# A hybrid decoder step on one core: grouped table matmuls, a regrouped state-space schedule, and unscaled query norms with fused scores

## The chip, the cores and the metric

The kernel runs on one core of one Trainium2 chip. It is written engine by engine: TensorE (PE in the profile) multiplies, VectorE (DVE), ScalarE (ACT) and GpSimd (POOL) work on tiles, SyncE (SP) issues most DMAs. Every engine works through its own queue in order, and semaphores make an instruction wait for what it reads or overwrites. The metric is the device time of one launch in microseconds.

## What is computed

One inference step of a decoder layer for 256 prompt positions and 8 x 4 sample positions, 288 columns in all, in float32:

```python
x = x + 0.5 * swiglu(rms_norm(x), w_gate, w_up, w_down)  # FFN 1
z = rms_norm(x) @ w_in  # columns: ssm u | q | k | v
# SSM: 64 groups x 16 channels, 64 complex states a group
lam_bar = exp(lam * dt);  B_bar = ((lam_bar - 1) / lam) * B
h[t] = lam_bar * h[t-1] + B_bar u[t];  y = gelu(Re(C h) + D u)
y = y * sigmoid(y @ w_glu)
# attention: 16 query heads, 4 key heads, window 128, one sink a head
q = rms_norm(q); k = rms_norm(k)
logits = where(valid, q k^T / 8 - slope * distance, -inf)
m = max(max(logits), sink)
p = exp(logits - m); o = (p @ v) / (sum(p) + exp(sink - m))
x = x + w_out @ concat(rms_norm(y_ssm), rms_norm(o))
x = x + 0.5 * swiglu(rms_norm(x), ...)  # FFN 2
```

The two norms in front of q can be joined: q's own norm divides by the root mean square of a head, so a common factor of the token (R, the norm of the layer's input) drops out of everything but the epsilon.

## The kernel before

**Bulk work.** All large products go through `mm3` (L290 to L292): the weights are split into a high part `wh` (ACT, L124) and a low part `wl` (DVE, L125), and each k tile takes three matmuls of 288 columns. The weights come as *pieces* in one list; a piece is used in one *slot* (24 matmuls in the projections). While TensorE works on a slot, the next pieces are split two slots ahead and loaded six ahead (`raw`, SP's queue).

**Side work.** Everything else is hung between the pieces. `W.at(slot, f)` runs f in the queue order of that slot; `W.spread(slot, generator)` runs one step of a generator a slot, up to each `yield`. So the engines' queues are written by this list, and an instruction of a later slot never overtakes one of an earlier slot on its engine. Small products use tiles of one PSUM pool, eight tiles named `main`, in rotation with the bulk work.

**Tables.** During FFN 1, `precompute` builds the SSM's matrices for eight j, one tile a turn, with `tile_tables` (L620 to L636): four transposes (L623) into a PSUM tile, a copy, a step; the same again; then one product of 128 rows by 256 columns (L629), of which only four diagonal blocks of 32 rows by 64 columns are used and copied out one by one (L636).

**The mixing stage** begins at slot `base`. Slots base to base+39 hold w_in: key 0, then the eight SSM blocks j (two slots each, from base+2), key 1, the values, and the query blocks i = 0 to 7 (from base+24); w_out follows from base+40.

An SSM block j passes through these steps, each in a slot of its own relation to s = base+2j+5: its input is stored to DRAM (`ud`, from ACT's queue) and loaded back in another layout (`ssm_u_load`, tile `U`, four DMAs of 36 KB, L767); its matrices come by `ssm_load_a` (`ma`, 512 KB, L771), `ssm_load_r` (`rot`, L775) and `ssm_load_b` (`mb`, 768 KB, L789), all in SP's queue; `ssm_state` multiplies (L798), rotates with `rot` on DVE (L804 to L807), scans (L814), rotates back (L820 on POOL, L821 on DVE); `ssm_out` multiplies again (L833). Then come the gate (`ssm_glu`, L856) and the split of the result for w_out (`y_split`, L737 to L747).

**Attention.** A query block i (two heads) is scaled by R out of PSUM (`qn`, L1171, DVE), squared (`q_square`, L1007, ACT), and summed by small matmuls (`sums`, L1025). `row_rsqrt` (L970 to L976) takes the reciprocal root on POOL, for two blocks at once. `scores` multiplies with the keys (L1043), scales by that root on ACT (L1049), adds the distance bias on DVE (L1053), takes the maximum (L986, L987), the exponentials on ACT (L994) and the final scale on DVE (L1002). `probs_t` transposes (L1062), `pv` multiplies with the values (L1075) and copies the head out (L1079). `sample` does the same for the 32 sample tokens (L1093 to L1142).

The slots of the attention's steps are written by hand, in relation to S, the slot at which block i's query is there (`probs_t` at S+9, `pv` at S+11).

## Time and profile before

| what | value |
|---|---|
| median of three runs | 1873.59 us (1873.23 to 1874.56) |
| the profiled execution | 1872.55 us |
| its span | 1870.7 us |
| TensorE busy | 1852.7 us (99%) |
| DVE, ACT, POOL busy | 1211.4, 852.0, 249.7 us |

In the trace FFN 1 runs to about 806 us, the mixing stage from there to about 1060, and FFN 2 after it. "Waits" below are idle times of an engine, put down to the instruction that released it. In the chain of work that ended last, a row is the start, the length and the instruction or DMA. In a group of instructions the columns are line, engine, operation, output and inputs, shapes and count, then the busy time and the mean of one in ns, then the idle time before it. A float32 matmul other than a transpose shows as two records.

### The profile page before, as it was taken

Reading aid. Unit: us, or ns where it says so; the run is one execution under the profiler, and the core shown is the slowest. Engines: PE = TensorE matmul, PEld = TensorE weight load, DVE = VectorE, ACT = ScalarE, POOL = GpSimd, SP = SyncE. Lnnn points to the kernel's source line nnn. Section 1 sums busy time; section 2 is a strip of 40 time slices with the busy share of each in tenths; the row PEclk is TensorE's granted clock in tenths of the full one; section 3 lists DMA queues with packets and bytes.
Section 4 is the critical chain, followed back from the end, with each engine's and each line's share of the span. In section 5 each row is a group of like instructions: output and inputs, shape, how many; then the busy total and the mean of one; then the engine's idle time right before and its main releaser. Section 6 shows DMA issues by size and latency. Waiting matters only on the chain.

```text
span 1870.7 us, 38190 instructions
## 1 busy us (share of the span) xinstructions
PE 1852.7 (99%) x15620; PEld 1836.0 (98%) x15620; DVE 1211.4 (65%) x1893; ACT 852.0 (46%) x1347; POOL 249.7 (13%) x324
## 2 busy tenths in 40 slices
PE   9999999999999999999989999999999999999999
PEld 9999999999999999998989999999999999999999
DVE  6677667666667755688888885555555555555555
ACT  6444444444444444643576554443444334434433
POOL 3201011000100100211214740000000000000000
PEclk9999999999999999999999999999999999999999
DMA  7555656557655764788734455556555565556555
GB/s 278 199 181 163 219 181 212 193 164 234 207 197 154 235 214 148 234 296 293 237 123 140 157 181 183 179 159 189 191 179 168 171 197 180 162 169 208 180 161 161
DMA packets 122624, 359.08 MB, mean 192 GB/s; under 512 B 22064, under 2 KB 30256, under 8 KB 121264
## 3 DMA queue, kind: packets, MB, share of 16 engines
q1 hardware_dynamic: 114496, 340.48, 56.7%
q10 hardware_dynamic: 7952, 16.16, 2.5%
q8 instruction: 122, 2.00, 0.4%
q14 instruction: 54, 0.44, 0.1%
HBM read 338.40 MB, written 20.22 MB: 192 GB/s over the span
## 4 chain that ended last, share of the span: by engine, by line
PE 92%; DVE 3%; DMA 2%; issue 1%; ACT 1%; POOL 1%; SPq 0%; DVEq 0%; ACTq 0%; POOLq 0%
PE main L290 30%; PE main L292 30%; PE main L291 30%; DVE wl L125 1%; DMA U<-ud 1%; DMA ud<-t 0%; DMA raw<-in_w_in 0%; DMA yd<-yg 0%; PE main L623 0%; PE main L629 0%; ACT wh L124 0%; PE main L833 0%; PE main L1062 0%; DVE sm_m L986 0%; POOL x L1178 0%
## 5 line engine op out<-in xcount | busy, mean ns | idle before, releaser
L125 DVE TENSOR_TENSOR wl<-raw,wh 128x1024 fp32r<-128x1024 f32 (+2 forms) x677 | 753.5, 1113 | 442.9 <-ACT wh L124 441.2
L290 PE MATMUL main<-xh,wh 128*128 128x288 f32 x3136 | 903.5, 288 | 0.4 <-ACT xh L216 0.3
L292 PE MATMUL main<-xh,wl 128*128 128x288 f32 x3136 | 898.6, 287 | 0.7 <-DVE wl L125 0.6
L291 PE MATMUL main<-xl,wh 128*128 128x288 f32 x3136 | 898.1, 286 | 0.9 <-DVE xl L217 0.9
L124 ACT CAST wh<-raw 128x1024 fp32r<-128x1024 f32 (+2 forms) x677 | 637.2, 943 | 493.3 <-PE main L291 332.7
L290 PEld LDWEIGHTS main<-xh,wh 128*128 128x128 f32 x3136 | 593.4, 189 | 3.6 <-ACT xh L216 0.8
L291 PEld LDWEIGHTS main<-xl,wh 128*128 128x128 f32 x3136 | 593.4, 189 | 1.9 <-DVE xl L217 1.5
L292 PEld LDWEIGHTS main<-xh,wl 128*128 128x128 f32 x3136 | 593.4, 189 | 1.7 <-DVE wl L125 0.8
L290 PE MATMUL main<-hh,wh 128*128 128x288 f32 x1664 | 477.8, 287 | 0.0
L291 PE MATMUL main<-hl,wh 128*128 128x288 f32 x1664 | 476.0, 286 | 0.6 <-DVE hl L743 0.6
L292 PE MATMUL main<-hh,wl 128*128 128x288 f32 x1664 | 476.0, 286 | 0.0
L291 PEld LDWEIGHTS main<-hl,wh 128*128 128x128 f32 x1664 | 314.5, 189 | 1.0 <-DVE hl L743 0.8
L290 PEld LDWEIGHTS main<-hh,wh 128*128 128x128 f32 x1664 | 314.5, 189 | 0.3
L292 PEld LDWEIGHTS main<-hh,wl 128*128 128x128 f32 x1664 | 314.5, 189 | 0.2 <-DVE wl L125 0.2
L364 POOL TENSOR_TENSOR s<-s,R 128x288 f32<-128x288 f32 x88 | 70.5, 801 | 1139.7 <-ACT s L363 1139.7
L373 ACT CAST hh<-h 128x288 fp32r<-128x288 f32 x88 | 38.0, 432 | 222.3 <-DVE h L372 222.3
L363 ACT ACTIVATE s<-t 128x288 f32<-128x288 f32 x88 | 39.0, 443 | 219.5 <-DVE t L362 219.5
L394 DVE SCALAR_TENSOR_TENSOR x<-main,x 128x288 f32<-128x288 f32 x128 | 58.4, 456 | 39.8 <-PE main L292 39.4
L372 DVE TENSOR_TENSOR h<-main,s 128x288 f32<-128x288 f32 x88 | 40.1, 456 | 55.2 <-PE main L292 54.9
L362 DVE TENSOR_TENSOR t<-main,R 128x288 f32<-128x288 f32 x88 | 40.1, 456 | 44.9 <-PE main L292 44.6
L374 DVE TENSOR_TENSOR hl<-h,hh 128x288 fp32r<-128x288 f32 x88 | 40.4, 459 | 43.8 <-ACT hh L373 43.8
L1178 POOL TENSOR_TENSOR x<-x,t 128x288 f32<-128x288 f32 x32 | 47.8, 1499 | 52.0 <-DVE t L1177 51.2
(262 smaller groups left out, 818.1 us busy)
## 6 DMA issues: line engine op xcount, KB each, us to landing
raw<-in_w_gu SPq DMA_DIRECT2D x349, 512.0 KB, 4.1
raw<-in_w_dn SPq DMA_DIRECT2D x128, 384.0 KB, 3.1
raw<-in_w_dn SPq DMA_DIRECT2D x128, 320.0 KB, 3.2
raw<-in_w_in SPq DMA_DIRECT2D x40, 512.0 KB, 4.7
raw<-in_w_out SPq DMA_DIRECT2D x32, 512.0 KB, 3.5
...
ma<-mats SPq DMA_DIRECT2D x8, 512.0 KB, 5.7
```

The costliest lines, as they stand in the source:

```text
L124: self.nc.scalar.copy(wh[:, :n], t[:, :n])
L125: self.nc.vector.tensor_tensor(wl[:, :n], t[:, :n], wh[:, :n].bitcast(F32), op=ALU.subtract)
L290: pe.matmul(ps, wh[:, s], woven(rh[k]), start=first and a == 0, stop=False)
L291: pe.matmul(ps, wh[:, s], woven(rl[k]), start=False, stop=False)
L292: pe.matmul(ps, wl[:, s], woven(rh[k]), start=False, stop=last and a == n - 1)
L362: dve.tensor_tensor(t1, pg[:, :N], R, op=ALU.mult)
L363: act.activation(s1, t1, AF.Silu)
L364: pool_e.tensor_tensor(s2, s1, R, op=ALU.mult)
L372: dve.tensor_tensor(halved(h), evens(pu[:, :N]), evens(s2), op=ALU.mult)
L374: dve.tensor_tensor(hl, h, hh.bitcast(F32), op=ALU.subtract)
L394: dve.scalar_tensor_tensor(x[d], ps[:, :N], 0.5, x[d], op0=ALU.mult, op1=ALU.add)
L1178: eng.tensor_tensor(x[d], x[d], t, op=ALU.add)
```

## The change

**Tables.** One group a tile: eight transposes into two PSUM tiles, then the product as eight matmuls of 32 output rows and 64 columns, each onto its own column tile (its 32 PSUM partitions), so that only the diagonal blocks are computed. One copy takes all four blocks. A tile takes two steps fewer.

**SSM.** State j is one piece later and stands between the same two pieces as out j-2, ahead of it. `ma` and `rot` of j > 1 are loaded one slot later than before, and U ahead of them. DVE's four products of 256 columns become two of 512; POOL's product (L820) goes to DVE; the subtraction and addition follow in the same step. Two gate blocks run in the same slots. The SSM's norm starts in the same slot, with one step a slot where it had two.

**Attention.** q is no longer scaled by R: DVE copies it out of PSUM, and ACT squares it from PSUM. The epsilon then has to carry the token's sum of squares, which `eps_rows` puts in place (three matmuls of two columns, some small copies). `bias` writes distance times slope, divided by the root, on ACT, in four copies a head block, from SBUF. `scores` comes two slots later (i even) or three (i odd); one fused DVE operation a part adds that bias to the PSUM scores, multiplies by the root, and takes the maximum with the sink. Four of them, each with a read of its maximum, replace ACT's four scaling copies and DVE's two additions, two reductions and one maximum.

```diff
@@ -617,23 +617,21 @@
+            pss = [pa.tile([P, 512], F32, name="main") for _ in range(3)]
             for i in range(2):
-                ps = pa.tile([P, 512], F32, name="main")
                 for q_ in range(4):
-                    pe.transpose(ps[:, q_ * P:(q_ + 1) * P],
+                    pe.transpose(pss[i][:, q_ * P:(q_ + 1) * P],
                                  bed[i][:, q_].rearrange("p j g c -> p (j g c)"), ident)
-                act.copy(stage[:, i].rearrange("p q m -> p (q m)"), ps)
-                yield
-            ps = pa.tile([P, 512], F32, name="main")
             for i, xx in ((0, xr), (1, xi)):
-                pe.matmul(ps[:, :256], rep[i].rearrange("p q g c -> p (q g c)"), xx[:, :, 1:5, :],
-                          start=i == 0, stop=i == 1)
+                for q_ in range(4):
+                    pe.matmul(pss[2][32 * q_:32 * q_ + 32, :64], rep[i][:, q_].rearrange("p g c -> p (g c)"),
+                              xx[:, q_, 1:5, :], start=i == 0, stop=i == 1)
+            act.copy(stage[:, 0].rearrange("p q m -> p (q m)"), pss[0])
             yield
-            for q_ in range(4):
-                pp = slice(32 * q_, 32 * q_ + 32)
-                act.copy(kk[pp].rearrange("p n d -> p (n d)"), ps[pp, 64 * q_:64 * q_ + 64])
+            act.copy(kk.rearrange("p n d -> p (n d)"), pss[2][:, :64])
...
+    def eps_rows():
+
+        a = acc.rearrange("p (j t) -> p j t", j=T)
+        pool_e.tensor_copy(vT[:, 0, :SEQ].rearrange("p (b j k) -> p j b k", b=2, j=T),
+                           a[:, :, NB:].rearrange("p j (b k) -> p j b k", b=2))
+        r = vT[:, 1, :P].rearrange("p (b g j) -> p j g b", b=NB, g=4)
+        for j in range(T):
+            pool_e.tensor_copy(r[:, j], a[:, j, None, :NB].to_broadcast([P, 4, NB]))
+        yield
+        ps = aux()
+        for b, rows in enumerate((vT[:, 0, :P], vT[:, 0, P:SEQ], vT[:, 1, :P])):
+            pe.matmul(ps[:, 2 * b:2 * b + 2], rows, e["ones"][:, :2], start=True, stop=True)
+        v = mp.tile([P, 6], F32, name="eps_v")
+        ts(v, ps[:, :6], EPS / D, EPS * EPS, op0=ALU.mult, op1=ALU.add)
+        yield
+        pool_e.tensor_copy(eps_q[:, 0:4], v[:, 0:4])
+        pool_e.tensor_copy(eps_q[:, 4:10], v)
...
-        br, bi = b[0][:, :, NB:], b[1][:, :, NB:]
-        co, si = rot[:, :, 0, :], rot[:, :, 1, :]
-        z, w = (sa.tile([P, 2, 4, NCH], F32, name="r" + n, bufs=2) for n in "zw")
+        both = [P, 2, 4, NCH]
+        cosi = rot.rearrange("p q s k -> p s q k")
+        co, si = cosi[:, 0], cosi[:, 1]
+        z, w = (sa.tile(both, F32, name="r" + n, bufs=2) for n in "zw")
         q = slice(4 * j, 4 * j + 4)
-        tt(z[:, 1], br, co, op=ALU.mult)
-        tt(w[:, 1], bi, si, op=ALU.mult)
-        tt(z[:, 0], bi, co, op=ALU.mult)
-        tt(w[:, 0], br, si, op=ALU.mult)
-        yield
+        for r, v in ((z, b[0]), (w, b[1])):
+            tt(r, v[:, None, :, NB:].to_broadcast(both), cosi, op=ALU.mult)
         for i in range(2):
             tt(fin_s[:, i, q, :], b[i][:, :, :NB], fin_s[:, i, q, :], op=ALU.add)
-        tt(z[:, 1], z[:, 1], w[:, 1], op=ALU.add)
-        tt(z[:, 0], z[:, 0], w[:, 0], op=ALU.subtract)
+        yield
+        tt(z[:, 0], z[:, 0], w[:, 1], op=ALU.add)
+        tt(z[:, 1], w[:, 0], z[:, 1], op=ALU.subtract)
         for i in range(2):
             dve.tensor_tensor_scan(flat(w[:, i]), flat(D0[j % 2]), flat(z[:, i]), 0.0, op0=ALU.mult, op1=ALU.add)
         yield
         cs = CS[j % 2]
-        for i in range(2):
-            act.copy(cs[:, i, :, :NB], e["h0"][:, 1 - i, q, :])
-        both = [P, 2, 4, NCH]
-        pool_e.tensor_tensor(z, w, si[:, None].to_broadcast(both), op=ALU.mult)
+        act.copy(cs[:, :, :, :NB], e["h0"][:, :, q, :])
+        tt(z, w, si[:, None].to_broadcast(both), op=ALU.mult)
         tt(cs[:, :, :, NB + 1:], w, co[:, None].to_broadcast(both), op=ALU.mult)
-        yield
-        tt(cs[:, 1, :, NB + 1:], cs[:, 1, :, NB + 1:], z[:, 0], op=ALU.subtract)
-        tt(cs[:, 0, :, NB + 1:], cs[:, 0, :, NB + 1:], z[:, 1], op=ALU.add)
+        tt(cs[:, 0, :, NB + 1:], cs[:, 0, :, NB + 1:], z[:, 1], op=ALU.subtract)
+        tt(cs[:, 1, :, NB + 1:], cs[:, 1, :, NB + 1:], z[:, 0], op=ALU.add)
+        yield
         act.copy(fin[:, :, q], cs[:, :, :, W1])

...
+    W.spread(base + 4, eps_rows())
...
-        W.at(s + 1 if j > 1 else base + 1 + j, ssm_load_a, j)
-        W.at(s + 1 if j > 1 else base + 2 + j, ssm_load_r, j)
         W.at(s + 2, ssm_u_load, j)
-        W.at(s + 2, ssm_decay, j)
-        W.spread(s + 4, ssm_state(j), True)
+        W.at(s + 2 if j > 1 else base + 1 + j, ssm_load_a, j)
+        W.at(s + 2 if j > 1 else base + 2 + j, ssm_load_r, j)
+        W.at(s + 3, ssm_decay, j)
         W.at(s + 6, ssm_load_b, j)
-        W.at(s + 9, ssm_out, j)
-        if j % 2:
-            W.at(s + 10, ssm_y_store, j // 2)
-            W.at(s + 11, ssm_y_load, j // 2)
-            W.spread(s + 13, ssm_glu(j - 1))
-            W.spread(s + 14, ssm_glu(j))
-    W.at(s + 8, state_done)
-    W.at(s + 17, ssm_done)
-
...
+    for j in range(10):
+        s = base + 2 * j + 10
+        if j < 8:
+            W.spread(s, ssm_state(j))
+        if j > 1:
+            W.at(s, ssm_out, j - 2)
+        if j in (3, 5, 7, 9):
+            y = (j - 3) // 2
+            W.at(s + 1, ssm_y_store, y)
+            W.at(s + 2, ssm_y_load, y)
+            s += 6 if y < 3 else 5
+            W.spread(s, ssm_glu(2 * y))
+            W.spread(s, ssm_glu(2 * y + 1))
+    W.at(base + 28, state_done)
+    W.at(base + 36, ssm_done)
+    W.spread(base + 38, e["norm"](e["ones"], acc, R_ssm, 1.0 / 1024, 4 * EPS))
...
-    def q_square(i):
-        qb = QN[i]
-        sq = mp.tile([P, SEQ], F32, name="qsq", bufs=2)
-        act.activation(sq, qb, AF.Square)
-        QN[i] = (qb, sq)
-        p, g = divmod(i, 4)
-        if g == 3:
-            s2 = mp.tile([P, P], F32, name="qssq")
-            qs = QS[p][0].rearrange("p b g j -> p (b g j)")
-            act.activation(s2, qs, AF.Square)
-            act.activation(qs, qs, AF.Copy, scale=qg)
-            QS[p] = (qs, s2)
+    def q_scale(p):
+        qs = QS[p].rearrange("p b g j -> p (b g j)")
+        act.activation(qs, qs, AF.Copy, scale=qg)
...
-        ts(v, ps[:, :cols], 1.0 / 64, EPS, op0=ALU.mult, op1=ALU.add)
-        RQ[m] = row_rsqrt(v, cols)
+        stt(v, ps[:, :cols], 1.0 / 64, eps_q[:, :cols], op0=ALU.mult, op1=ALU.add)
+        vs = mp.tile([P, 8], F32, name="rq_s", bufs=2)
+        tt(vs, v[:, :8], nsl[:, 8 * m:8 * m + 8], op=ALU.mult)
+        o = row_rsqrt(v, cols)
+        pool_e.tensor_tensor(vs, vs, o[:, :8], op=ALU.mult)
+        RQ[m] = o, vs
+
+    def bias(i):
+        lg = L[i] = late["a"].tile([P, 2, 384], F32, name="lg", bufs=3)
+        nb = RQ[i // 2][1][:, 4 * (i % 2):4 * (i % 2) + 4]
+        for blk, (lo, hi) in enumerate(((0, 128), (128, 384))):
+            for hb in range(2):
+                c = 2 * blk + hb
+                act.activation(lg[:, hb, lo:hi], dist[:, lo:hi], AF.Copy, scale=nb[:, c:c + 1])

     def scores(i):
         p, g = divmod(i, 4)
         qb, sq = QN.pop(i)
-        rq = RQ[i // 2][:, 4 * (i % 2):4 * (i % 2) + 4]
+        rq = RQ[i // 2][0][:, 4 * (i % 2):4 * (i % 2) + 4]
...
-        yield
-        lg = L[i] = late["a"].tile([P, 2, 384], F32, name="lg", bufs=3)
-        for hb in range(2):
-            for blk, (lo, hi) in enumerate(((0, 128), (128, 384))):
-                act.activation(lg[:, hb, lo:hi], pss[hb][:, lo:hi], AF.Copy,
-                               scale=rq[:, 2 * blk + hb:2 * blk + hb + 1])
-        yield
-        for hb in range(2):
-            stt(lg[:, hb], dist, -SLOPES[heads_of(i)[hb]], lg[:, hb], op0=ALU.mult, op1=ALU.add)
-        yield from softmax(lg, ((0, 128), (128, 384)), sinkp[:, 4 * i:4 * i + 4], 4)
+        lg, sink, parts = L[i], sinkp[:, 4 * i:4 * i + 4], ((0, 128), (128, 384))
+        m, es_, l = (mp.tile([P, 4], F32, name="sm_" + n, bufs=4) for n in "mel")
+        for blk, (lo, hi) in enumerate(parts):
+            for hb in range(2):
+                c = 2 * blk + hb
+                dve.tensor_tensor_reduce(lg[:, hb, lo:hi], pss[hb][:, lo:hi], lg[:, hb, lo:hi], rq[:, c:c + 1],
+                                         sink[:, c:c + 1], ALU.add, ALU.max, m[:, c:c + 1])
+        tt(es_, sink, m, op=ALU.subtract)
+        ts(m, m, -1.0, None, op0=ALU.mult)
+        yield
+        yield from exps(lg, parts, m, es_, l)
...
-        W.at(s, q_square, i)
         W.at(s + 11, pv, i)
+        if i % 4 == 3:
+            W.at(s + 1, q_scale, i // 4)
     for m in range(4):
         W.at(S[2 * m + 1] + 1, sums, m)
-    for i in range(8):
-        W.spread(S[i | 1] + 1 + i % 2, scores(i))
+    for i, s in enumerate(S):
+        W.at(S[i | 1] + 3 + i % 2, bias, i)
+        W.spread(S[i | 1] + 3 + i % 2 * 2, scores(i))
...
-        QN[i] = mp.tile([P, SEQ], F32, name="qn", bufs=4)
-        tt(blocks(QN[i]), prompt(ps[:, :N]), prompt(R), op=ALU.mult)
-        tt(QS[p][0][:, :, g, :].rearrange("p b j -> p j b"), tok(ps[:, :N], None), tok(R, None), op=ALU.mult)
+            QS[p] = mp.tile([P, NB, 4, T], F32, name="qs", bufs=2)
+            SQ[p] = mp.tile([P, P], F32, name="qssq")
+        sq = mp.tile([P, SEQ], F32, name="qsq", bufs=2)
+        s2 = SQ[p].rearrange("p (b g j) -> p g j b", b=NB, g=4)
+        act.activation(blocks(sq), prompt(ps[:, :N]), AF.Square)
+        act.activation(s2[:, g], tok(ps[:, :N], None), AF.Square)
+        qn = mp.tile([P, SEQ], F32, name="qn", bufs=4)
+        dve.tensor_copy(blocks(qn), prompt(ps[:, :N]))
+        dve.tensor_copy(QS[p][:, :, g, :].rearrange("p b j -> p j b"), tok(ps[:, :N], None))
+        QN[i] = (qn, sq)
```

Left out are the unpacking of results, the `cs` halves in `ssm_out` (both change places), constants (`nsl`, the slopes) and renamed indices.

How the queues change, at the three places where the following sections look. First SP's queue where the SSM's second and third blocks are loaded (`raw` a weight piece, `mats` the tables); before:

```order
L116 DMA raw<-in_w_in 128x1024
L771 DMA ma<-mats_128 128x1024
L775 DMA rot<-mats_128 128x512
L116 DMA raw<-in_w_in 128x1024
L789 DMA mb<-mats_126 128x1536
L767 DMA U<-ud_10106 32x4x72 x4
L116 DMA raw<-in_w_in 128x1024
L771 DMA ma<-mats_129 128x1024
L775 DMA rot<-mats_129 128x512
```

and now:

```order
L116 DMA raw<-in_w_in 128x1024 x2
L807 DMA mb<-mats_126 128x1536
L785 DMA U<-ud_10130 32x4x72 x4
L789 DMA ma<-mats_128 128x1024
L793 DMA rot<-mats_128 128x512
L116 DMA raw<-in_w_in 128x1024 x2
L807 DMA mb<-mats_127 128x1536
L785 DMA U<-ud_10131 32x4x72 x4
L789 DMA ma<-mats_129 128x1024
```

A block's `U` stood behind its own `ma` and `rot`, a weight piece and the `mb` of two blocks earlier. It still stands behind that `mb`, but ahead of its own `ma` and `rot`, which have moved down by a weight piece.

Second, TensorE's queue around one state group. Before, the group of block j (`U`, `ma`) stood alone between bulk matmuls:

```order
L291 MATMUL main<-xl_111,wh 128x288
L292 MATMUL main<-xh_94,wl 128x288
L798 MATMUL main<-U,ma 64x72 x16
L290 MATMUL main<-xh_95,wh 128x288
L291 MATMUL main<-xl_112,wh 128x288
L292 MATMUL main<-xh_95,wl 128x288
```

Now the out group (`mb`) of the block two earlier follows it directly:

```order
L292 MATMUL main<-xh_102,wl 128x288
L816 MATMUL main<-U,ma 64x72 x16
L848 MATMUL main<-U,mb 64x72 x2
L848 MATMUL main<-cs_10192,mb 64x72 x4
L848 MATMUL main<-U,mb 64x72 x2
L848 MATMUL main<-cs_10192,mb 64x72 x4
L848 MATMUL main<-U,mb 64x72 x2
L848 MATMUL main<-cs_10192,mb 64x72 x4
L848 MATMUL main<-U,mb 64x72 x2
L848 MATMUL main<-cs_10192,mb 64x72 x4
L290 MATMUL main<-xh_87,wh 128x288
```

The state group is one piece (24 bulk matmuls) later than it was, and the bulk matmuls between it and the out group are gone.

Third, DVE's queue at the first head of the attention. Before:

```order
L861 SCALAR_TENSOR_TENSOR s_11922<-s_11833,yn 128x288
L125 TENSOR_TENSOR wl<-raw,wh 128x1024
L1053 SCALAR_TENSOR_TENSOR lg<-mcst,lg 128x384 x2
L986 TENSOR_REDUCE sm_m<-lg 128x2 x2
L987 TENSOR_TENSOR sm_m<-sm_m,sinks 128x4
L988 TENSOR_TENSOR sm_e<-sinks,sm_m 128x4
L989 TENSOR_SCALAR sm_m<-sm_m 128x4
L743 SCALAR_TENSOR_TENSOR hl<-s_11874,gains,hh 128x288
```

and now (each `ISA` row with `lg` is the fused operation, each row with one column the read of its maximum):

```order
L125 TENSOR_TENSOR wl<-raw,wh 128x1024 x2
L1072 ISA lg,sm_m<-main,lg,sinks,rq_o 128x128
L1072 ISA sm_m 128x1
L1072 ISA lg,sm_m<-main,lg,sinks,rq_o 128x128
L1072 ISA sm_m 128x1
L1072 ISA lg,sm_m<-main,lg,sinks,rq_o 128x256
L1072 ISA sm_m 128x1
L1072 ISA lg,sm_m<-main,lg,sinks,rq_o 128x256
L1072 ISA sm_m 128x1
L1074 TENSOR_TENSOR sm_e<-sinks,sm_m 128x4
L1075 TENSOR_SCALAR sm_m<-sm_m 128x4
```

Two additions, two reductions and three small operations have become four fused operations with four reads and two small operations; the copies `lg<-main` on ACT that stood before them are gone from ACT's queue, and four copies from SBUF stand there two slots later.

More of the change, by code (lines that the diff above doesn't have):

```diff
@@ L633, in tile_tables @@
             km = qp.tile([P, 4, 2, 16], F32, name="km")
-            for q_ in range(4):
-                pp = slice(32 * q_, 32 * q_ + 32)
-                act.copy(kk[pp].rearrange("p n d -> p (n d)"), ps[pp, 64 * q_:64 * q_ + 64])
+            act.copy(kk.rearrange("p n d -> p (n d)"), pss[2][:, :64])
+            act.copy(stage[:, 1].rearrange("p q m -> p (q m)"), pss[1])
             yield
@@ L706, in aux @@
         return pa.tile([P, 512], F32, name="main")
-    cst = mp.tile([P, P + 384 + 160 + 6], F32, name="mcst")
+    cst = mp.tile([P, P + 384 + 160 + 38], F32, name="mcst")
     sinks = mp.tile([P, 36], F32, name="sinks")
-    bones, dist, dist_s, nslope, even, odd = (cst[:, a:b] for a, b in (
-        (0, 128), (128, 512), (512, 672), (672, 676), (676, 677), (677, 678)))
+    bones, dist, dist_s, nslope, even, odd, nsl = (cst[:, a:b] for a, b in (
+        (0, 128), (128, 512), (512, 672), (672, 676), (676, 677), (677, 678), (678, 710)))
     sinkp, sinks_s = sinks[:, 0:32], sinks[:, 32:36]
@@ L722, in mix @@
     yd = [dr.tile([2 * P, N], F32, name="yd%d" % j) for j in range(4)]
+    eps_q = mp.tile([P, 10], F32, name="eps_q")
+    def eps_rows():
[14 more added lines that the diff above has]
+        pool_e.tensor_copy(eps_q[:, 4:10], v)
     def consts():
@@ L830, in ssm_out @@
         for q in range(4):
-            for a, rhs in enumerate((u[:, q], cs[:, 1, q, :W1], cs[:, 0, q, :W1])):
+            for a, rhs in enumerate((u[:, q], cs[:, 0, q, :W1], cs[:, 1, q, :W1])):
                 for hh in HALVES:
@@ L921, in k_norm @@
         yield
-        kT = tp.tile([P, N], F32, name="s1")
+        kT = tp.tile([P, N], F32, name="h")
         stt(kT, kr, gains[:, 65:66], rk, op0=ALU.mult, op1=ALU.mult)
@@ L961, in mix @@
         W.at(W.i + 3, v_rows, p)
-    QN, L, PT, CK, CV, QS, YR, RQ = ({} for _ in range(8))
+    QN, L, PT, CK, CV, QS, SQ, YR, RQ = ({} for _ in range(9))
     def row_rsqrt(v, w):
@@ L1089, in sample @@
     def sample(p):
-        qs, sq = QS.pop(p)
-        rq = RQ[2 * p + 1][:, 8:10]
+        qs = QS.pop(p).rearrange("p b g j -> p (b g j)")
+        rq = RQ[2 * p + 1][0][:, 8:10]
         rqe, rqo = (mp.tile([P, 2], F32, name="rq_" + n) for n in "ab")
@@ L1168, in mix @@
         if g == 0:
-            QS[p] = (mp.tile([P, NB, 4, T], F32, name="qs", bufs=2),)
-        QN[i] = mp.tile([P, SEQ], F32, name="qn", bufs=4)
-        tt(blocks(QN[i]), prompt(ps[:, :N]), prompt(R), op=ALU.mult)
-        tt(QS[p][0][:, :, g, :].rearrange("p b j -> p j b"), tok(ps[:, :N], None), tok(R, None), op=ALU.mult)
+            QS[p] = mp.tile([P, NB, 4, T], F32, name="qs", bufs=2)
[8 more added lines that the diff above has]
+        QN[i] = (qn, sq)
     def add_x(d, ps, r, eng):
@@ L1243, in constants @@
     bones = np.kron(np.eye(2, dtype=f), np.ones((64, 64), f))
-    mix = np.concatenate([bones, dist, dist_s, ns, 1 - b[:, None] % 2, b[:, None] % 2], 1)
+    sl = np.array([-SLOPES[heads_of(i)[c % 2]] for i in range(8) for c in range(4)], f)
+    mix = np.concatenate([bones, dist, dist_s, ns, 1 - b[:, None] % 2, b[:, None] % 2, np.tile(sl, (P, 1))], 1)
     return cst, np.ascontiguousarray(mix.astype(f)), np.eye(P, dtype=f)
@@ L1329, in unlayout @@
     for i in range(2):
-        out.append(unpair(r["fin"][:, 1 - i]).reshape(1, 1, 64, 64))
+        out.append(unpair(r["fin"][:, i]).reshape(1, 1, 64, 64))
     for n, new in (("old_k", ks), ("old_v", vs)):
```

8 lines of the change are left out of this document (3 added, 5 removed).

## The prediction

> **What bounds the kernel now.** I read the page's totals first, then the busy time by stage, then who TensorE waits for.
>
> ```profile
> span 1870.7 us, 38190 instructions
> PE 1852.7 (99%) x15620; PEld 1836.0 (98%) x15620; DVE 1211.4 (65%) x1893; ACT 852.0 (46%) x1347; POOL 249.7 (13%) x324
> ```
>
> TensorE is busy for 99% of the span, so a change pays only where it takes TensorE time away: its own small matmuls, its waits, or time at a lower clock. The engines' totals say nothing about single stages. The windows do; the columns are the stretch and its length, then busy time and count of PE, PEld, DVE, ACT and POOL, then the granted clock, DMA share and GB/s:
>
> ```profile
> 806.00:880.00 74.00, 70.25 (x778) 67.34 (x776) 63.90 (x118) 26.30 (x44) 10.92 (x7) 0.98 0.85 290
> 880.00:925.00 45.00, 43.75 (x569) 40.77 (x569) 39.98 (x77) 21.21 (x47) 10.12 (x9) 1.00 0.81 268
> 925.00:980.00 55.00, 49.54 (x472) 46.08 (x470) 43.68 (x121) 38.18 (x107) 12.76 (x41) 1.00 0.42 137
> 980.00:1036.00 56.00, 55.55 (x542) 52.40 (x543) 44.79 (x92) 38.40 (x110) 25.20 (x32) 0.97 0.40 133
> ```
>
> 806 to 925 is the SSM stage: DVE is busy 86 to 89% of it and the DMA engines 81 to 85%. 925 to 1036 is the attention: DVE 79 to 80%, ACT 69%, DMA light. Between 806 and 1036 TensorE is idle for 3.75 + 1.25 + 5.46 + 0.45 = 10.9 us. The waits view names nearly all of it (total, times, longest):
>
> ```profile
> PE main L798 <- DMA U<-ud: 4.8, 3, 2.6
> PE main L1025 <- ACT qsq L1007: 2.3, 1, 2.3
> PE main L1100 <- ACT lg L1049: 2.0, 1, 2.0
> PE main L1062 <- ACT s L1079: 1.6, 1, 1.6
> ```
>
> The SSM's U loads cost 4.8, the attention's three waits 5.9. Two of these waits cost more than they last:
>
> ```profile
> 872.00:876.00 4.00, 2.47 (x38) 2.43 (x39) 4.00 (x6) 0.58 (x3) 1.00 (x1) 0.86 0.93 305
> 876.00:880.00 4.00, 4.00 (x24) 3.62 (x22) 0.41 (x2) 0.00 (x0) 0.00 (x0) 0.71 0.98 356
> 948.00:952.00 4.00, 1.99 (x26) 1.40 (x26) 1.19 (x5) 2.33 (x7) 1.91 (x8) 1.00 0.74 261
> 980.00:984.00 4.00, 3.55 (x31) 3.31 (x32) 3.86 (x10) 3.97 (x15) 0.00 (x0) 0.59 0.40 125
> ```
>
> Behind the longest U wait (2.6) the granted clock falls to 0.86 and 0.71: 0.14 x 4 + 0.29 x 4 = 1.7 us of full-speed work lost. Behind the 2.3 us wait it is 0.59, 1.6 us lost. Behind the 2.0 us wait it stays 1.00. So a wait between 2.0 and 2.3 us is where a second bill begins in this trace.
>
> The Trainium skill, "TensorE: Matmul & The Clock Gate", Part 1, says that the clock halves after at least one idle window of about 3.4 us; by it neither wait would do, and the 3.3 us would stay (about 1862.8, a rival below). The rows differ, and the measurement decides.
>
> **The SSM tables (precompute).** Per tile now, for eight tiles:
>
> ```profile
> 203.23 0.44 PE main L623 x4
> ...
> 205.88 0.86 PE main L629 x4
> ```
>
> Two groups of four transposes and one 128x256 product: 0.44 + 0.44 + 0.86 = 1.74 us. The transposes stay, so 0.88 stays. The product becomes 8 matmuls of 32 output rows and 64 columns, on four column tiles. Two float32 records each, as now, makes 16 records of a quarter of the 256 columns. No row has this shape; bounds come from the nearest two:
>
> ```profile
> 842.38 0.29 PE L292 MATMUL main<-xh,wl 128*128 128x288 f32 x1
> 842.60 1.22 PE L798 MATMUL main<-U,ma 128*64 128x72 f32 x32
> ...
> 843.97 0.29 PE L291 MATMUL main<-xl,wh 128*128 128x288 f32 x1
> ...
> 846.67 0.29 PE L292 MATMUL main<-xh,wl 128*128 128x288 f32 x1
> ...
> 848.76 0.29 PE L291 MATMUL main<-xl,wh 128*128 128x288 f32 x1
> ```
> ```profile
> 993.53 0.59 PE main L1104 x16
> ```
>
> The first fence is the timeline around a state group (32 records, two column tiles) and an out group (48 records). A bulk matmul starts every 0.1225 us. From 842.38 to 843.97 are 1.59 us, less the two bulk matmuls among them: 1.345 us for 32 records. From 846.67 to 848.76: 1.845 us for 48. So a record costs 0.5/16 = 0.031 us, and going into and out of the narrow form 1.345 - 32 x 0.031 = 0.345 us per group. Sixteen records at 0.031 give 0.5 + 0.345 = 0.845: almost nothing saved (-0.02 a tile, -0.2 in all). If four tiles run side by side, the time is that of 16 records x 0.216 x 64/256 / 4 = 0.216 + 0.345 = 0.56: -0.3 a tile, -2.4 in all. L1104, narrow tiles too, puts sixteen records of 256 columns into 0.59; one by one, at 0.86/4 = 0.216 each, they would take 3.5. So such tiles do run side by side. I take 0.60: **-2.1 us**. Two steps fewer a tile only shorten a queue whose engines wait for TensorE.
>
> **The SSM's groups.** State j now stands in the same gap between pieces as out j-2, six times. Each saves one entry and exit: 6 x 0.345 = **-2.1** (if the group's second half has to wait for its operands, nothing is saved; ends 0 and -2.1).
>
> **The U loads.** Why TensorE waits there, from the chain, and the price of a neighbour in SP's queue, from the page (KB, us to landing):
>
> ```profile
> 861.93 7.91 DMA raw<-in_w_in
> ...
> 869.86 3.38 DMA U<-ud
> ...
> 873.53 1.22 PE main L798 x32
> ```
> ```profile
> ma<-mats SPq DMA_DIRECT2D x8, 512.0 KB, 5.7
> ```
>
> U was held in SP's queue until a weight load had landed, then took 3.38 us. The change gives state j one piece (24 x 0.1225 = 2.94 us) more after the same issue slot of U, and sets U's four loads ahead of ma and rot, not behind them. ma and rot go one slot later but are needed one slot later, so their lead stays at three slots, 8.8 us against 5.7. The three waits (longest 2.6) are each shorter than 2.94, so by this all 4.8 + 1.7 = 6.5 us go. Against it: DMA share 0.81 to 0.85 over the stage and 0.93 to 0.98 in the windows above, so moved bytes push others; and if ma is late next, TensorE waits as before. Ends 0 and -6.5; I let one wait of 1.2 us stay: **-5.3**.
>
> DVE must not get later there. POOL's multiply goes to DVE (one pair from the timelines, then the group of eight, least/median/most ns):
>
> ```profile
> 845.55 2.18 POOL L820 TENSOR_TENSOR rz<-rw,rot 128x512 f32<-128x512 f32 x1 [6.30 <-DVE rw L814]
> 846.50 1.77 DVE L821 TENSOR_TENSOR cs<-rw,rot 128x512 f32<-128x512 f32 x1
> L821 DVE TENSOR_TENSOR cs<-rw,rot x8: 679/1224/1775, 838.0 to 912.6; 128x512 f32<-128x512 f32 x8
> ```
>
> DVE's product beside it took 1.77 while POOL's ran, and 0.679 at the least; the median is 1.224. With POOL quiet, two products cost 2 x 0.68 = 1.36 a state, 0.14 more than now; four products of 256 become two of 512, which spares two starts. I count DVE as unchanged. Were the 0.14 paid on top, 8 x 0.14 = 1.1 us would lie on an engine with 11 to 14% idle.
>
> **The attention.** Scores of one head on DVE, from the chain:
>
> ```profile
> 934.13 0.95 DVE lg L1053 x2
> 935.10 1.02 DVE sm_m L986 x2
> ...
> 980.45 0.41 PE main L1025 x8
> ```
> ```profile
> L1171 DVE TENSOR_TENSOR qn<-main,R 128x256 f32<-128x256 f32 x8 | 3.3, 417 | 2.2 <-PE main L292 2.2
> L1114 DVE SCALAR_TENSOR_TENSOR ls<-main,rq_b,ls 128x128 f32<-128x128 f32 x4 | 1.4, 343 | 0.0
> ```
>
> 0.95 + 1.02 and the three tiny operations behind make about 2.5 us. Four fused operations take their place, each followed by a read of its maximum. The operation is not in this trace. Nearest: 0.343 (128 columns, one PSUM source) and 0.417 (256), so 2 x 0.343 + 2 x 0.417 = 1.52, plus two tiny operations, 1.9; with a read as long as a tiny operation 2.5. I take 2.2 a head, DVE a little freer.
>
> Of the three waits: the 2.3 us one is a square that waited for DVE's scaled query. The square now reads PSUM on ACT, so the wait and its 1.6 of slow clock go (-3.9). The 2.0 us one:
>
> ```profile
> 938.55 1.28 ACT L994
> ...
> 940.15 1.56 ACT lg L994 x7
> 941.81 0.94 ACT wh L124
> ...
> 949.42 0.22 POOL rq_o L976
> ```
> ```profile
> 949.67 1.35 ACT L1049 ACTIVATE lg<-main,rq_o 128x128 f32<-128x128 f32 x4 [2.90 <-POOL rq_o L976]
> ```
>
> ACT stood before the scale copies until POOL's norm was ready at 949.6, with the sample's matmul behind it for a PSUM tile. Scores now come two slots (5.9 us) later, and no ACT copy reads their PSUM: -2.0. The 1.6 us wait (PSUM tile until ACT has copied the head's output) is untouched. What is late next: the four bias copies (1.35, the price of the four scale copies that went) now stand in ACT's queue ahead of the table load (1.28) and the eight exponentials and reads (1.56 for seven, so 1.8): 4.4 us, with two weight casts of 0.94 6.3, where two slots have 5.9: 0.4 too many before the SSM's squares, which stand there too. The weight cast behind them, and DVE's subtraction that waits for it, then delay the first head's end of softmax, for which probs waits. Between 0 and one slot (2.9): I take 1.4. So -3.9 - 2.0 + 1.4 = **-4.5** (ends 0 and -5.9 unless the 1.6 goes too, -7.5).
>
> The three small matmuls of the new epsilon rows cost about 0.4 (L1025's eight took 0.41), joining scores to neighbouring groups gives about 0.5 back: -0.1, ends +0.4 and -0.5.
>
> **Sum.** -2.1 - 2.1 - 5.3 - 4.5 - 0.1 = -14.1. The profiled execution took 1872.55 us (span 1870.7 and 1.85 around it), so 1858.4; the median of the three runs, 1873.59, is 1.04 above it, so I forecast **1859.5**.
>
> **Rivals.** (a) The SSM stage is bound by transfers: at 0.93 to 0.98 busy, U's gain is ma's or mb's loss, and 2 of the 6.5 us go: +3.3, 1862.8; with the column tiles at their dear end 1864.7. (b) ACT's queue in the first heads decides: the new wait recurs for a second pair and passes 2.3 us, so it brings a slow clock (1.6): the attention gains nothing or loses 3: 1864 to 1867. (c) The slow clock has another cause than the wait before it: 3.3 us stay, 1862.8; both cases here speak against it. (d) (a) and (b) together, the column tiles at their dear end: 1869 to 1872. (e) Slower: the fused operation. DVE has 11.3 us idle between 925 and 980, of which 5.5 lie in TensorE's waits; 5.9 over some six heads (my estimate of those that pass in that stretch) is 1.0 us a head. So up to 3.5 us a head is hidden; each microsecond above it costs 8. The forecast's 14.1 is eaten at 3.5 + 14.1/8 = 5.3 a head, 1.25 an operation with its read, as dear as L821's median above. At 1.4 an operation it is 1879. For it speaks only that the operation is unseen.
>
> **Chances.** Forecast 0.46, its own range 1855 to 1863; (a) 0.19; (b) 0.14; (c) 0.04; (d) 0.09; (e) 0.08. All ends at their best (-2.4 - 2.1 - 6.5 - 7.5 - 0.5 = -19.0) give 1854.6, the low end, rounded to 1854; the high end, 1869, takes in (b) with the column tiles at nothing and leaves out (d) and (e), 0.17. A measurement of this kernel tells about 0.2% (3.7 us) from no change: faster is the forecast with (a), (b) and (c), 0.83; within it (d), 0.09; slower (e), 0.08.
>
> **What would show it.** Tables: the chain shows the new group behind eight transposes at about 0.6, not 0.85. SSM: no wait for U in the waits view, the granted clock 1.00 from 872 on, state and out as one group; wrong if ma, rot or mb stand in U's place. Attention: no wait of L1025's successor for squares, none of the sample's scores; the fused groups on DVE at 0.35 to 0.45, and one wait of 1 to 2 us at a probs transpose. A second stretch at half clock, or DVE over 90% busy from 925 to 980, would make the prediction wrong.

## The result, and the profile after

| kernel | runs | median | lowest to highest |
|---|---|---|---|
| before | 6 | 1873.8 us | 1872.98 to 1877.76 |
| changed | 6 | 1863.02 us | 1860.05 to 1867.76 |

The ratio is 0.9943, with a 95% interval of 0.9930 to 0.9956: 0.57% faster, 10.7 us of 1873.8 (8.2 to 13.1). The forecast was 1859.5, 14.1 less than before.

The changed kernel's six times spread over 7.7 us (the six of before over 4.8, 26 later ones of before over 8.0), and its profiled execution, 1867.47 us, is one of the longer ones. So terms are read from its profile, and the size of the whole from the runs. Two slow runs are left out of all ratios: one of 2126.34 us at a mean clock of 0.85 (the store of y later) and one of before of 3937.17 us. The page's totals after:

```profile
span 1865.7 us, 38408 instructions
PE 1850.2 (99%) x15722; PEld 1834.1 (98%) x15722; DVE 1203.2 (64%) x1914; ACT 845.5 (45%) x1321; POOL 243.4 (13%) x327
```

The windows of the same four stretches (length, busy time and count of PE, PEld, DVE, ACT, POOL, then granted clock, DMA share, GB/s):

```profile
806.00:880.00 74.00, 69.96 (x819) 68.23 (x819) 61.45 (x113) 26.56 (x40) 2.90 (x8) 0.98 0.84 277
880.00:925.00 45.00, 45.00 (x555) 42.73 (x551) 38.08 (x80) 20.09 (x47) 6.04 (x12) 1.00 0.87 293
925.00:980.00 55.00, 52.44 (x501) 49.06 (x501) 44.33 (x138) 42.94 (x128) 16.63 (x42) 0.97 0.42 141
980.00:1036.00 56.00, 55.22 (x542) 51.88 (x541) 44.81 (x101) 36.80 (x97) 29.24 (x35) 1.00 0.44 141
```

The waits view of TensorE (total, times, longest):

```profile
PE main L816 <- DMA ma<-mats: 3.9, 1, 3.9
PE main L1085 <- ACT s L1102: 2.0, 1, 2.0
...
PE main L1085 <- DVE lg L1021: 1.0, 2, 0.5
```

The three waits for U have become one wait for ma, of 3.9 us. Of the attention's three waits, the squares' and the sample's are gone; the wait of a probs transpose (L1085, which was L1062) for the copy of a head's output is there still, 2.0 where it was 1.6, and new ones of 1.0 in all wait for the final scale (L1021). The waits for ma and for the copy have a slow clock behind them, and the start of the program has one too, which before did not show:

```profile
12.00:16.00 4.00, 4.00 (x19) 4.00 (x20) 4.00 (x7) 3.42 (x6) 0.00 (x0) 0.57 1.04 413
...
876.00:880.00 4.00, 3.59 (x70) 3.62 (x72) 2.56 (x6) 1.68 (x3) 0.00 (x0) 0.58 1.02 387
...
956.00:960.00 4.00, 2.81 (x15) 2.82 (x16) 3.50 (x14) 1.99 (x4) 1.03 (x6) 0.74 0.59 200
```

For a view by stage that clocks and waits do not blur, I take the starts of all matmuls in a trace, sum the distances from each to the next over a range of slots, and subtract 0.1225 us for each bulk matmul. What is left is the stage's **excess**: small matmuls, waits and slow clock together. Slots count from base.

| kernel, profiled | FFN 1 after its start | slots 8-25 (SSM) | 29-39 | 40-71 |
|---|---|---|---|---|
| before | 15.1 | 31.4 | 19.1 | 22.4 |
| changed | 12.6 | 26.9 | 18.8 | 20.4 |
| changed, again | 12.6 | 26.3 | 18.9 | 20.4 |
| tables only | 12.6 | 33.5 | 19.1 | 23.8 |
| SSM only | 15.0 | 23.6 | 21.6 | 21.4 |
| attention only | 15.0 | 32.3 | 15.4 | 21.4 |
| mats first | 12.6 | 24.4 | 17.2 | 20.4 |
| gates apart | 12.6 | 23.1 | 18.8 | 20.4 |
| odd bias on POOL | 12.6 | 23.5 | 15.3 | 20.0 |
| ... and mats first | 12.6 | 30.8 | 15.3 | 19.9 |
| ... and y later | 12.6 | 28.2 | 15.3 | 19.9 |
| ... and both | 12.6 | 26.0 | 15.3 | 19.9 |
| odd bias on POOL, fewer bytes | 11.9 | 21.6 | 15.3 | 22.1 |

From before to changed these are -2.5, -4.5, -0.3 and -2.0. With +2.6 in the first 25 slots (7.9 before, 10.5 after), +0.7 in slots 0 to 7 (the epsilon rows) and +1.0 in slots 26 to 28 (a gate group that moved there) they give the -5.1 between the two profiled executions. The +2.6 at the start belongs to the execution: on the other rows the same first slots cost 8.0 to 9.9 (9.9 in the second profile of the changed kernel, which has a slow clock there too, 0.62).

### The profile page after: what moved, and what is told of

It is laid out like the page before. It is cut to its first block, busy times and chain, and to the rows that moved or that the text cites. A ratio compares the mean times of both kernels' runs of the same rounds, so it can differ in the third digit from the quotient of the medians.

```text
span 1865.7 us, 38408 instructions
## 1 busy us (share of the span) xinstructions
PE 1850.2 (99%) x15722; PEld 1834.1 (98%) x15722; DVE 1203.2 (64%) x1914; ACT 845.5 (45%) x1321; POOL 243.4 (13%) x327
## 4 chain that ended last, share of the span: by engine, by line
PE 92%; DVE 3%; DMA 2%; ACT 1%; issue 1%; POOL 0%; SPq 0%; ACTq 0%; DVEq 0%; POOLq 0%
PE main L290 30%; PE main L292 30%; PE main L291 30%; DVE wl L125 1%; DMA ma<-mats 1%; ACT wh L124 1%; PE main L848 0%; DMA yd<-yg 0%; PE main L623 0%; PE main L816 0%; DMA raw<-in_w_gu 0%; DMA ud<-t 0%; POOL x L1209 0%; PE main L871 0%; ACT lg L1013 0%
```

## The experiments

Each was timed against the kernel before on its own chip; ratios have 95% intervals.

**The changed kernel again, and each part alone.** The three parts are the hunks of the diff on the tables, on the SSM (with the key's `kT` buffer) and on the attention (with the epsilon rows), each put into the kernel before. For the kernel again:

> The changed kernel itself, once more. Its six runs fell into 1860 to 1861 and 1865 to 1868, and the profiled one (1867.5) has a 3.9 us wait for ma with 1.4 us of half clock, a 1.96 us wait in the attention with 1.7 us of half clock, and a start that is 2.5 us longer than that of before. Theory A (these three are chances of an execution, the rest is fixed): the runs spread by several us again, and a profile near 1860 lacks the wait for ma. Theory B (the waits belong to the schedule, the spread to the chip): a profile near 1860 to 1862 still has the ma wait and the attention's, and differs at the start only.

Measured: 1865.52 us (1861.14 to 1868.67), ratio 0.9949 (0.9936 to 0.9963). The profile, of 1866.5 us, has the wait for ma again, 2.9 us, and the attention's, 1.98 us, with its slow clock. No profile near 1860 came of this kernel, so A and B are not told apart here; but the two waits are no accident of one execution. The spread is there again: the twelve runs of both sets lie between 1860.05 and 1868.67.

> The kernel before with the tables part of the change alone. From the two traces: 1.744 us a tile before, 1.431 after, so 8 x 0.313 = 2.5 us less, about 0.9987. The rival (column tiles one after the other, or the two steps fewer a tile shift other side work) gives 0 to 1 us.

Measured: 0.9987 (0.9979 to 0.9996), 2.4 us less. As expected from the traces.

> The kernel before with the SSM part alone. Mine: six merged groups 2.1 us less, the U waits with their slow clock 6.5 us less, so about 8.6 us (0.9954), or about 3.3 us (0.998) in executions in which ma is late by 3.9 us with its slow clock. Rival: the wait for transfers only moves, always 2 to 3 us in all (0.9987).

Measured: 0.9976 (0.9966 to 0.9987), 4.5 us less: between the two cases and above the rival. Its waits:

```profile
PE main L1097 <- ACT lg L1046: 3.6, 1, 3.6
PE main L798 <- DMA ma<-mats: 1.8, 1, 1.8
```

U is gone and ma is late, as in the full change. What I had not expected is the first line: with the SSM regrouped, the old attention's wait for the sample's scores grew from 2.0 to 3.6 us. Its slots 29 to 39 cost 21.6 where they cost 19.1 before. About 1.7 us of that are a slow clock behind the wait, which the old wait of 2.0 did not have.

> The kernel before with the attention part alone. Mine: 2.5 us less (0.9987) as in the profiled execution of the change, to 4.5 us (0.9976) as predicted, if no stretch at half clock follows the 1.96 us wait for the copy of a head's output. Rival: the bias copies on ACT cost as much as the removed wait gave, 0 to 1 us.

Measured: 0.9978 (0.9969 to 0.9986), 4.1 us less, near the upper end. The wait for the copy of a head's output is 1.5 us there, no slow clock follows, and slots 29 to 39 cost 15.4, 3.7 less than before. In the full change the same slots cost 18.8. So the parts do not simply add up inside a stage: the SSM's regrouping takes 3.4 us of the attention's gain back in the profiled executions, while the ratios of the three parts, 0.13 + 0.24 + 0.22 = 0.59%, come near the whole by the runs.

**What takes it back in the attention.** The chain of the changed kernel shows ACT without a pause ahead of the late copy:

```profile
950.94 0.90 ACT wh L124
951.84 1.39 ACT lg L1055 x4
...
953.82 1.17 ACT lg L1013 x5
...
955.93 0.93 ACT wh L124
956.86 0.28 ACT s L1102
957.14 0.04 issue
957.18 0.55 PE main L1085 x3
```

A weight cast, four bias copies (1.39), exponentials, a weight cast, and only then the copy (L1102) that frees the PSUM tile. Two edits ask which of the things ahead of it counts. Gates apart (the second of a pair one slot later than in the change):

```diff
-            W.spread(s, ssm_glu(2 * y + 1))
+            W.spread(s + 1, ssm_glu(2 * y + 1))
```

> The changed kernel with the second gate block of a pair one slot behind the first, as they stood before. In the profile of the change ACT works without a pause from 945.7 to 957.2, two gated splits (1.7 us) among it, and the head's copy (L1102) for which TensorE waits 1.96 us stands at the end of that. Theory C (the burst of the gates): the wait falls to 1.4 us or less, as with the attention part alone, and the 1.5 us of half clock behind it go: 2 to 3 us less than the change. Rival D (the bias copies alone fill ACT): the wait stays at 1.8 to 2.0 with its slow clock, the time is that of the change within 1 us.

Measured: 0.9958 (0.9944 to 0.9972), from twelve runs of 1861.5 to 1873.68. Slots 29 to 39 stay at 18.8:

```profile
PE main L1085 <- ACT s L1102: 2.1, 1, 2.1
PE main L816 <- issue: 1.4, 1, 1.4
```

The wait is 2.1 us, with its slow clock. The burst of the two gates is not the cause. (The second line is ma again: it landed at 871.57, 0.2 us ahead of L816.) The odd bias on POOL:

```diff
-                act.activation(lg[:, hb, lo:hi], dist[:, lo:hi], AF.Copy, scale=nb[:, c:c + 1])
+                if i % 2:
+                    pool_e.tensor_scalar(lg[:, hb, lo:hi], dist[:, lo:hi], nb[:, c:c + 1], None, op0=ALU.mult)
+                else:
+                    act.activation(lg[:, hb, lo:hi], dist[:, lo:hi], AF.Copy, scale=nb[:, c:c + 1])
```

> The changed kernel with the bias of every second head block on POOL, not ACT. Rival D (bias copies fill ACT's queue): the four copies ahead of the late one (1.4 us) go, the 1.96 us wait falls to 0.6 or less and the slow clock behind it goes: 3 us less than the change. Theory C (the gates): also less wait, by the same 1.4 us, but the gates' part stays; C and D are told apart by the experiment before. Against both: POOL's copies are slow (a 128x256 multiply takes it 1.2 to 1.5 us) and the fused operation then waits for POOL: the time rises by 1 to 3 us.

Measured: 1860.56 us (1858.88 to 1861.8), ratio 0.9929 (0.9916 to 0.9942).

```profile
PE main L816 <- DMA ma<-mats: 1.8, 1, 1.8
...
PE main L1088 <- ACT s L1105: 1.0, 1, 1.0
```

The wait is 1.0 (0.6 was expected), the slow clock behind it is gone, and the stage costs 15.3, 3.5 less, as it did with the attention part alone. POOL takes 0.86 and 0.96 us a copy on average, and no engine waits for them in this list. So the four bias copies in ACT's queue made the copy later by 1.0 of its 2.0 us. They are not what the SSM's regrouping adds: with the attention part alone they stand in that queue too, and the wait is 1.5 there, without a slow clock. Of the 3.4 us that the regrouping takes back, 1.6 are the slow clock (the row "mats first", where none followed the same wait, has 17.2) and 1.0 are longer waits: 2.0 where it was 1.5, and 0.5 for the final scale, which is new there. What lengthens these waits in the regrouped schedule no run isolates. This version's runs are within 2.9 us of each other. Its interval and those of the changed kernel (0.9930 to 0.9956 and 0.9936 to 0.9963) overlap, so it is the fastest full version here by its median, but not shown faster than the change by the runs alone; what speaks for it is the stage's excess, in one profile of it and two of the change.

**What makes ma late.** The chain of the changed kernel ahead of the 3.9 us wait:

```profile
861.38 7.16 DMA yd<-yg
...
868.60 0.33 SPq L807
...
868.97 0.86 SPq L785
...
871.37 4.84 DMA ma<-mats
876.21 0.20 issue
876.41 1.67 PE main L816 x23
```

and SP's own waits, of before (806 to 900) and after (806 to 880):

```profile
SPq L767 <- DMA yd<-yg: 11.6, 3, 7.7
```
```profile
SPq L807 <- DMA yd<-yg: 6.4, 1, 6.4
```

SP issued mb (L807) only after a part of the store of y, which ACT had issued, had landed; then came U's four loads and ma. (mb reads nothing that this store writes; why SP's issue waits for it, the traces do not say.) Before, the same store held U. Two theories: A, the order of loads behind a held queue decides; B, the transfers of the stage as a whole are too many for it, and one of them is late in any order. Mats first, in one slot of SP's queue:

```diff
-        W.at(s + 2, ssm_u_load, j)
         W.at(s + 2 if j > 1 else base + 1 + j, ssm_load_a, j)
         W.at(s + 2 if j > 1 else base + 2 + j, ssm_load_r, j)
+        W.at(s + 2, ssm_u_load, j)
         W.at(s + 3, ssm_decay, j)
-        W.at(s + 6, ssm_load_b, j)
+        if j > 1:
+            W.at(s + 2, ssm_load_b, j - 2)
```

(with mb of blocks 6 and 7 in the slots they had).

> The changed kernel with another order in one slot of SP's queue: ma and rot of block j, then its U, then mb of block j-2 (the change has mb, U, ma, rot). In both profiles of the change SP stood 4.8 to 6.4 us until the y store (yd<-yg, issued by ACT) had landed, then issued mb, four U pieces, and ma 2.3 to 2.8 us later; ma landed 2.9 to 3.9 us late. Theory A (order behind a held queue): ma is issued about 2.2 us earlier and shares the engines with less, the wait for ma goes, and what waits next is U or mb by at most 1.5 us: 2 to 3.5 us less than the change. Rival B (transfers are the bound, whatever the order): the wait only changes its name, 2 to 4 us for U or mb, the time is that of the change within 1 us.

Measured: 0.9950 (0.9935 to 0.9966), that of the change. The wait changed its name, as B says: mb by 1.7 us in all, U by 0.3; the SSM's excess, 24.4, is some 2 us lower in this one execution, but gates apart, with the order of the change, has 23.1.

The store of y one slot later:

```diff
-            W.at(s + 1, ssm_y_store, y)
-            W.at(s + 2, ssm_y_load, y)
+            W.at(s + 1 + (y < 3), ssm_y_store, y)
+            W.at(s + 2 + (y < 3), ssm_y_load, y)
```

> The changed kernel with the store and the load of y one slot later (three of four). Theory A (the held queue): SP no longer waits for yd<-yg ahead of that mb, so mb, U and ma are issued some 3 us earlier and the wait for ma falls below 1 us: 3 to 5 us less than the change; another wait may appear where the store now stands. Rival B (transfers are the bound): ma is late by 2 us or more all the same.

No wait can be read from its one profile, which is of the run of 2126.34 us; the other four runs, 1863.21 to 1867.33, give 0.9951 (0.9937 to 0.9965), that of the change. To see past the attention's wait, the next three stand on the version with the odd bias on POOL.

> Odd bias on POOL (the experiment before) together with ma and rot ahead of U and mb. With the odd bias on POOL alone ma was 1.8 us late; with mats first alone mb was late by 1.7 us in all, at two places. Theory A (order behind a held queue): the waits shrink to 1 us or less, since mb is needed 1.3 us after ma: 0 to 2 us less than with the odd bias on POOL alone (1858.5 to 1860.5). Rival B (transfers are the bound): 1.5 to 2.5 us of waits for mb or U, the same time within 1 us.

Measured: 1864.65 us, 0.9945 (0.9932 to 0.9959).

```profile
PE main L816 <- DMA U<-ud: 3.8, 2, 2.6
PE main L848 <- DMA mb<-mats: 2.4, 2, 1.2
```

U is late again, and mb too: 6.2 us, more than ever. A falls for this order.

> Odd bias on POOL together with the store and load of y one slot later (three of four). Theory A (the y store's landing holds SP's queue ahead of mb, U and ma): SP does not wait for yd<-yg at that place, ma is issued 2 us or more earlier and is in time: no wait of TensorE for ma, 1.8 us less than with the odd bias on POOL alone. Rival B (transfers are the bound): ma is still late by 1.5 us or more.

Measured: 1862.47 us, 0.9934 (0.9921 to 0.9947). Waits of TensorE, then of SP:

```profile
PE main L816 <- DMA ma<-mats: 3.9, 2, 3.4
```
```profile
SPq L785 <- DMA yd<-yg: 5.3, 1, 5.3
```

The wait for ma is 3.9 us at two places (the longer 3.4), where the base version had 1.8: the store now holds U's load in mb's place. A falls here too.

> All three: odd bias on POOL, ma and rot ahead of U and mb, y one slot later. Theory A: no wait for U, ma or mb over 0.5 us in the SSM stage, its cost beyond the bulk matmuls about 21.7 us, the time 1857 to 1860. Rival B: 1.5 us or more of such waits remain whatever the order, 1860 to 1862.

Measured: 1861.37 us, 0.9930 (0.9916 to 0.9944). mb 1.8, the load of y (L871 waits for yn) 1.4, U 0.6: 3.8 us of waits. Whatever the order, some load comes late, by 1.4 to 6.2 us in the profiles with the SSM regrouped. So B fits all these profiles, and the last run asks what the stage has too much of. Bytes, in the same DMAs and the same order:

```diff
-        MB[j] = sm.tile([P, 3, 4, P], F32, name="mb", bufs=2)
-        get(MB[j].rearrange("p a q m -> p (a q m)"), e["mats"][j][:, 1024:2560])
+        if j < 2:
+            MB[j] = MBS[j] = sm.tile([P, 3, 4, P], F32, name="mb%d" % j)
+        MB[j] = MBS[j % 2]
+        c = 1536 if j < 2 else 192
+        get(MB[j].rearrange("p a q m -> p (a q m)")[:, :c], e["mats"][j][:, 1024:1024 + c])
```

and the same for ma, 128 columns of 1024.

> Odd bias on POOL, with fewer bytes in the same DMAs: from the third block on, ma loads 64 KB where it loaded 512, and mb 96 KB where it loaded 768; the rest of both keeps the tables of an earlier block, so the SSM's numbers are those of other tables. The list of DMAs, their order and the instructions of all engines stay. Rival B1 (bytes are the bound of the stage): 1.1 of some 3.1 MB a block go, TensorE waits for no table and no U over 0.5 us, the stage's cost beyond the bulk matmuls is about 21.7 us as against 23.5 to 30.8, the time 1857 to 1859. Rival B2 (the queue is the bound: few DMAs in flight, each issue waiting for the landing of an earlier one, y and u stores of 72 and 144 KB taking 5 to 7 us): SP still stands before mb until yd<-yg has landed, and TensorE waits 1.5 us or more.

Measured: 1856.49 us (1855.79 to 1858.16), ratio 0.9908 (0.9892 to 0.9925). In the stage no load makes TensorE wait, and its excess is 21.6 (21.7 was expected). The windows from 822 to 900, with all bytes on POOL's version, and with fewer:

```profile
822.00:900.00 78.00, 76.19 (x1001) 73.90 (x1000) 69.82 (x135) 30.30 (x54) 4.11 (x4) 1.00 0.91 297
```
```profile
822.00:900.00 78.00, 78.00 (x1046) 75.21 (x1044) 71.10 (x137) 32.30 (x61) 3.82 (x4) 1.00 0.77 231
```

At a DMA share of 0.91 TensorE lost 1.8 us of these 78 to waits, at 0.77 nothing. So fewer bytes remove the waits, as B1 says. SP's stand before mb, 6.6 us for the store of y with all bytes, is gone as well, where B2 had it stay. This is one profile, and the two versions' intervals overlap (0.9892 to 0.9925 and 0.9916 to 0.9942); but all four runs lie below all five with all bytes (up to 1858.16, from 1858.88, on another chip). Still open is by which way the bytes make others late: a smaller DMA takes less of the 16 engines, and it also frees its place in the queue sooner, so that SP stands less. Both shrink together here, and no run parts them.

## Why the prediction came out as it did

**Tables, forecast -2.1.** Right, a little small. One group of the changed kernel in the timeline, between two bulk matmuls:

```profile
202.88 0.29 PE L292 MATMUL main<-hh,wl 128*128 128x288 f32 x1
203.00 1.04 PE L623 MATMUL main<-ident,bed 128*128 128x128 f32 x8
203.97 0.32 PE L627 MATMUL main<-xr,rep 128*32 128x64 f32 x8
204.10 0.29 PE L627 MATMUL main<-xi,rep 128*32 128x64 f32 x8
204.33 0.39 PE L290 MATMUL main<-hh,wh 128*128 128x288 f32 x1
204.56 0.29 PE L291 MATMUL main<-hl,wh 128*128 128x288 f32 x1
```

From 202.88 to 204.56, less two bulk matmuls, are 1.43 us, less 0.88 for the transposes 0.55 for the sixteen records: the bound for four column tiles side by side (0.56), where I took 0.60. 1.744 - 1.43 = 0.31 a tile, -2.5 in all, and the tables alone gave -2.4. The rival that the tiles do not run together is out.

**The SSM's groups, forecast -2.1.** Right. The state and out group in one:

```profile
854.81 0.29 PE L292 MATMUL main<-xh,wl 128*128 128x288 f32 x1
855.02 1.22 PE L816 MATMUL main<-U,ma 128*64 128x72 f32 x32
...
857.90 0.29 PE L291 MATMUL main<-xl,wh 128*128 128x288 f32 x1
```

857.90 - 854.81 - 0.245 = 2.845 us, where the two groups took 1.345 + 1.845: 0.345 less, the price of one entry and exit, six times.

**The U loads, forecast -5.3.** The mechanism was half right: U is in time now, at all three places. The step that failed is "ma and rot go one slot later but are needed one slot later, so their lead stays at three slots, 8.8 us against 5.7". The lead was counted in slots, from where the code puts the load; SP reached it late, since the DMA ahead of it was issued only after the store of y had landed. From its issue (871.37) to its need (876.41 less the wait of 3.9: 872.5) were 1.1 us, not 8.8. The rows for it were in the trace of before: SP waited 11.6 us for that store there. I had quoted the weight load that ended last in one chain, and taken it for the cause.

How much of the term is left differs by execution. From the change of slots 8 to 25 in the table I take the groups' -2.1 out and add the 1.0 that only moved to slots 26 to 28. The two profiles of the changed kernel then have -1.4 and -2.0 for this term, with ma 3.9 and 2.9 us late and a slow clock behind it. SSM only, gates apart and odd bias on POOL, which load in the same order, have -4.7, -5.2 and -4.8, with ma 1.4 to 1.8 us late and no slow clock. So the changed kernel's own profiles are rival (a), the SSM stage bound by transfers, which lets 2 us go, and the other three are near the forecast. That the measured 1863.0 is so near (a)'s 1862.8 is partly luck: the attention fell short too, and rival (c) has the same number. But (a)'s mechanism is what the last run supports.

DVE's part held: its products of 512 columns take 0.68 each now that POOL is quiet, and DVE's time between 806 and 925 fell from 103.9 to 99.5 us, though the two stretches do not hold quite the same work:

```profile
L836 DVE TENSOR_TENSOR cs<-rw,rot 128x512 f32<-128x512 f32 x8 | 5.4, 681 | 0.0
L835 DVE TENSOR_TENSOR rz<-rw,rot 128x512 f32<-128x512 f32 x8 | 5.4, 680 | 0.0
```

**The attention, forecast -4.5.** By slots 29 to 71 the profile gives -2.3 (18.8 + 20.4 against 19.1 + 22.4), by the part alone -4.1 from the runs. The two waits that were to go went. The fused operation was sized well:

```profile
L1072 DVE CUSTOM_DVE_ANT_0 lg<-main,lg,sinks 128x256 f32<-128x256 f32 x16 | 8.0, 538 | 0.0
L1072 DVE CUSTOM_DVE_ANT_0 lg<-main,lg,sinks 128x128 f32<-128x128 f32 x16 | 5.9, 402 | 0.0
L1072 DVE DVE_READ_ACCUMULATOR2_ANT sm_m<- 128x1 f32 x32 | 2.6, 80 | 0.0
```

The operation of 128 columns, 0.40, lies in the 0.35 to 0.45 I gave as a sign; that of 256, 0.54, lies above it. From the chain, a head's four operations begin at 941.79 and its last small one ends at 943.77: 2.0 us where 2.2 were taken and some 2.5 stood before. So rival (e), the slow fused operation, is out. What is late next was named rightly in kind (ACT's queue, behind the bias copies) but at the wrong instruction: not the first head's weight cast and softmax (1.0 us in all, forecast 1.4), but the copy of a head's output, called "untouched" at 1.6. It is touched, since four bias copies now stand ahead of it: 2.0 us. And the slow clock that I took as gone for good came back behind it (1.6 us), which is rival (b) in part. The epsilon rows, forecast at 0.4, cost 0.7 (slots 0 to 7).

**The slow clock.** "A wait between 2.0 and 2.3 us is where a second bill begins" was wrong. The same wait, 1.98 us in the changed kernel's second profile and 1.99 with mats first, was followed by these windows:

```profile
956.00:960.00 4.00, 3.73 (x19) 3.73 (x20) 3.83 (x17) 1.08 (x3) 1.69 (x9) 0.64 0.68 229
```
```profile
952.00:956.00 4.00, 3.79 (x30) 3.71 (x30) 3.83 (x17) 1.28 (x4) 1.75 (x9) 1.00 0.64 221
```

0.64 in the one, 1.00 in the other. So a wait of 2 us puts a slow clock at risk, and the length alone does not decide it. The Trainium skill, "TensorE: Matmul & The Clock Gate", Part 1, calls the window of about 3.4 us free-running, so that one kernel meets it in different phases from run to run; the pair above agrees with that. The Trainium skill's rule in the same Part 1, no idle gaps over about 3.4 us, is too wide for this case: a wait of 1.98 us was followed by a slow clock.

**Sum.** -2.4, -4.5 and -4.1 for the three parts make -11.0, the whole -10.7 (in the second set 0.9949, -9.5), the forecast -14.1; each part's interval is about 2 us to either side. The part with the largest shortfall is the SSM's: -4.5 where -7.4 was forecast. In its own profile, though, the SSM's slots gave -6.8 (31.4 to 23.6, with the 1.0 that moved), and slots 29 to 39, the attention, cost 2.5 more. That is the step the forecast left out: it added the SSM and the attention as if neither touched the other, and put the regrouping's effect on the attention at nothing, without a reason. In the profiles it was 2.5 us with the old attention and 3.4 with the new, 1.6 to 1.7 us of each the slow clock. Two of the signs that I had named came out against me, too: ma stood in U's place, and a slow clock followed two waits. The range, 1854 to 1869, held the time (the forecast's own, 1855 to 1863, ends right at it), and the sign came from three terms that each hold alone.
